# A scan's 32x32 inverse products broken into runs of 32 among projection matmuls

## The chip, the cores and the metric

The kernel runs on one core of a Trainium2 chip. The metric is the device time of one execution in microseconds, as the median of several executions.

## The reference

Four residual layers work on a sequence of 256 tokens of width 2048. Layers 0 and 3 are RWKV-7 time mixing, layer 1 is dilated attention, layer 2 a pooling mixer. Only the RWKV layers are touched. Cut to what matters:

```
def _rwkv7_mixer(h, ...):
    r, k, v, g = [(h + xx * mu[j]) @ w_in[j] for j in range(4)]
    decay = exp(-exp(w_log));  a = sigmoid(a0 + (xa @ a1) @ a2)
    kk = heads(k * k_k);  kk = kk / max(sqrt(sum(kk * kk)), 1e-12)
    k = k * (1 + (a - 1) * k_a)
    # S_t = S_{t-1} diag(w_t) + (S_{t-1} a_t) b_t^T + v_t k_t^T ;  y_t = S_t r_t
    y = _rwkv7_scan(r, decay, k, v, -kk, kk * a)
    y = _head_group_norm(y, lnx_w, lnx_b)
    bonus = sum(r * k * r_k, axis=-1) * v
    return ((y + bonus) * silu(g)) @ w_out
```

There are 32 heads of 64 channels. The recurrence over tokens is computed in 4 chunks of 64 tokens, and each chunk of each head needs the inverse of a 64x64 unit triangular matrix.

## The kernel before, in words

The four projections of an RWKV layer (r, k, v, g, each 2048 x 2048) are one long stream on TensorE. `linear` (L238) takes the weights in pieces of 512 KB: SyncE's queue loads `raw` (L190), ScalarE rounds it to `whi` (L193), VectorE makes the rest `wlo` (L194), and three matmuls of 256 columns per weight tile give a product (L284, tile `lin`). There are three buffers of each kind, and two pieces are fetched ahead. The inputs `xhi` and `xlo` (L169, L170) are made by `mix` from `hl`, read back from DRAM (L498, L502).

Everything else of the scan is written between the matmuls of that stream. `heads` and `group` are Python generators. After each step of six projection matmuls `linear` calls `tick`, which keeps a clock of its own: a generator yields (cost on TensorE in us, delay in us until its next piece may be written), or a letter for the stage it enters next and a condition for it. Stages A, S, D, C, E hold one generator each. A compiler pass then orders each engine's instructions by priority and by its own estimates. The engines work their lists in order and SyncE's queue is in order as well.

One `heads` generator handles a pair of blocks (4 heads): stage A makes decays and key norms (the products `z` L564, `ssp` L717), S the products inside a chunk (`sc` L771, L774; `tps` L796). Every second one goes on into `group` for 8 heads: stage D inverts, stage C runs the four chunks (`xps`, `ups`, `sps`, `yps`), E does the norm and the bonus (`gps` L970, `bps` L972, whose input `kb` is loaded at L967). A layer has 4 groups, the program 8.

In stage D the 16x16 diagonal blocks are inverted on VectorE, and TensorE joins them by products of 32x32 tiles: `prod` (L856, matmuls at L860) is called three times for tiles named `q`, then come `zp` (L876) and `pp` (L886). In `group` the second and third call stand back to back:

```
zp = prod(lambda o, n: NT[:, n, o % 64:o % 64 + 32], X0, 16)
yield 1.3, 2.0
...
xp = prod(lambda o, n: P0[:, n], Z, 32)
pp = prod(lambda o, n: Z[:, n], P0, 32)
yield 2.6, 2.5
```

A call of `prod` writes 64 matmuls of float32, and `zp` and `pp` 32 each. The trace records each such float32 matmul twice, so a call is 128 records there. A group's strictly triangular matrix `NT` has one buffer.

Of the kernel before, what the change touches and what calls it, by code (L numbers as in the profile page):

```python
# [9 lines left out]
F32 = mybir.dt.float32  # L10
F32R = mybir.dt.float32r
I32 = mybir.dt.int32
AF = mybir.ActivationFunctionType
ALU = mybir.AluOpType

P = 128
D = 2048
S = 256
# [4 lines left out]
C = 64  # L23
# [72 lines left out]
class Trunk:  # L96
# [482 lines left out]
    def rwkv(self, l, li):  # L579
        nc = self.nc  # L580
        a = self.i
        w2, srcs, have = {}, {}, (set(), set(), set(), set(), set(), set())
        self.omm = self.hid_pool.tile([P, 6 * KT], F32, name="omm")
        o = VIX[("mu", l, 0)] * KT
# [4 lines left out]
        io = lambda name: self.mp.tile([P, 2, S], F32, tag="io", name=name, bufs=4)  # L589
# [71 lines left out]
        with self.phase(f"scan{l}") as self.sp:  # L661

            grp = [[] for _ in range(KT // 4)]
            st = {"chunks": 0, "BK": False, "NT": None, "Y": False}
            self.queue += [(self.heads(l, li, pr, w2, srcs, have, grp[pr // 2], st),
                            lambda pr=pr: (2 * pr in have[0] and 2 * pr in have[1]
                                           and st["chunks"] >= pr // 2 - 1))
                           for pr in range(KT // 2)]
            for n, (m, lo, hi, rounds) in enumerate(self.order):
                xs = then[2]  # L670
                if n + 1 < len(self.order):
                    m2, lo2 = self.order[n + 1][:2]
                    then = (win(m2), lo2, self.mixer_inputs(l, m2), False)
                else:
                    then = (a["a_w_out"][l], 0,
                            lambda k: zs(k) if k // 2 * 2 in have[5] else None, True)
                self.part(win(m), lo, hi, xs, takes[m], rounds, then)
            self.drain()
# [3 lines left out]
    def heads(self, l, li, pr, w2, srcs, have, grp, st):  # L682


        nc, sp = self.nc, self.sp
        dma = nc.sync.dma_start
# [4 lines left out]
        j = 2 * pr  # L691

        sg = T("sg", [P, 4, S], 1)
        self.lora_out(sg[:, 0:2], w2["w"], j, srcs["w"], LORA_W, ("w0", l))
        self.lora_out(sg[:, 2:4], w2["a"], j, srcs["a"], LORA_W, ("a0", l))
        kt = T("kt", [P, 2, S], 1)
        dma(kt, self.kd[j // 2])
        yield 1.8, 1.5
        self.sigmoid_tail(sg)
        aa = sg[:, 2:4]  # L700
        Wi = T("Wi", [P, 2, S], 1)
# [10 lines left out]
        kk = T("kk", [P, 2, S], 1)  # L712
        for q in range(2):
            nc.scalar.activation(kk[:, q], kt[:, q], AF.Square, scale=self.col(("k_k", l), j + q))
        yield 0.0, 5.0
        ssp = self.ps.tile([P, 2, S], F32, tag="sm", name="ssp", bufs=2)
        nc.tensor.matmul(ssp.rearrange("p q t -> p (q t)"), self.cst("bd"),  # L717
                         kk.rearrange("p q t -> p (q t)"), start=True, stop=True)
# [12 lines left out]
        nc.vector.tensor_tensor(kp, kp, kt, op=ALU.mult)  # L731
        nc.vector.tensor_tensor(aa, aa, kk, op=ALU.mult)
        yield 0.9, 3.0
        while st["BK"]:
            yield 0.0, 1.0
        st["BK"] = True
        r = T("kt", [P, 2, S], 1)
        dma(r, self.rd[j // 2])
# [17 lines left out]

        mk = self.cst("smask")
        if pr % 2 == 0:
            while st["NT"] is not None:
                yield 0.0, 1.0  # L760
            st["NT"] = T("NT", [P, 16, C], 1)
        NT = st["NT"]
        n0 = pr % 2 * 8
        MR = T("MR", [P, 2, NC_, C], FLY)
        for q in range(2):
# [35 lines left out]
        st["BK"] = False  # L801
        grp.append((AR, MR, BT, Wc))
        if pr % 2:
            yield from self.group(l, li, pr // 2, have, grp, st)

    def group(self, l, li, gr, have, grp, st):

        nc, sp = self.nc, self.sp
        dma = nc.sync.dma_start
        T = lambda tag, shape, bufs: sp.tile(shape, F32, tag=tag, name=tag, bufs=bufs)  # L810
        half = (slice(0, 64), slice(64, 128))
        NT = st["NT"]

        yield "D", lambda: True
        ntd, pxd = self.ntd[gr % 2], self.pxd[gr % 2]
        for hh, rows in enumerate(half):
            dma(ntd[:, hh], NT[rows])
        Nb = T("Nb", [P, 16, 16], 1)
        for b in range(4):
            o = 16 * b  # L820
            dma(Nb[32 * b:32 * b + 32],
# [2 lines left out]
        px = px_.rearrange("p i (w t) -> p i w t", w=2)  # L824
        nc.scalar.copy(px[:, :, 0], self.cst("eye16").rearrange("p (i t) -> p i t", i=16))
        yield 0.0, 7.0
        tmp = T("tmp", [P, 64], 1)
        with self.tc.high_priority(PRIO_D):
            for i in range(15):
                w = 15 - i  # L830
# [14 lines left out]
        yield 0.0, 14.0  # L845

        rowm = self.cst("rows")
        PX = T("PX", [P, 16, 2, 32], 1)
        for o in range(2):
            nc.scalar.activation(PX[:, :, :, 16 * o:16 * o + 16],  # L850
                                 pc.rearrange("p (n w) t -> p n w t", w=2), AF.Copy,
# [1 line left out]
        P0, X0 = PX[:, :, 0], PX[:, :, 1]  # L853
        bank = lambda name: self.ps.tile([P, 16, 32], F32, tag="nt", name=name, bufs=2)

        def prod(fa, fb, kk_):  # L856
            q_ = bank("q")
            for n in range(16):
                for o in range(0, P, 32):
                    nc.tensor.matmul(q_[o:o + 32, n], fa(o, n)[o:o + kk_], fb[o:o + kk_, n],  # L860
                                     start=True, stop=True)
            return q_

        zp = prod(lambda o, n: NT[:, n, o % 64:o % 64 + 32], X0, 16)
        yield 1.3, 2.0
        Z = T("px", [P, 16, 32], 1)
        nc.scalar.activation(Z, zp, AF.Copy, scale=rowm[:, 1:2])
        xp = prod(lambda o, n: P0[:, n], Z, 32)
        pp = prod(lambda o, n: Z[:, n], P0, 32)
        yield 2.6, 2.5  # L870
        nc.vector.tensor_tensor(X0, X0, xp, op=ALU.add)
        nc.vector.tensor_tensor(P0, P0, pp, op=ALU.add)
        zp = bank("zp")
        for n in range(16):
            for b in (0, 64):
                nc.tensor.matmul(zp[b + 32:b + 64, n], NT[b:b + 32, n, 32:], X0[b:b + 32, n],  # L876
                                 start=True, stop=True)
        st["NT"] = None
        yield 1.0, 2.0
        Z2 = T("px", [P, 16, 32], 1)  # L880
        for b in (0, 64):
            nc.scalar.copy(Z2[b + 32:b + 64], zp[b + 32:b + 64])
# [1 line left out]
        for n in range(16):  # L884
            for b in (0, 64):
                nc.tensor.matmul(pp[b:b + 32, n], Z2[b + 32:b + 64, n], P0[b + 32:b + 64, n],  # L886
                                 start=True, stop=True)
        yield 1.0, 1.5
        yield "C", lambda: (4 * gr in have[2] and 4 * gr + 2 in have[2] and not st["Y"])
        Pm = T("P", [P, 16, C], 1)  # L890
        for o in range(2):
# [8 lines left out]
        def values(c):  # L900

            SV = T("SV", [P, 2, 2, 2, C], 2)
            UV = T("UV", [P, 2, 2, 2, C], 2)
            vc = vv[c * C:(c + 1) * C]
            for hh, rows in enumerate((half[1], half[0])):
                for t in (SV, UV):
                    dma(flat(t[rows, hh]), flat(vc[:, hh]))
            return SV, UV

        Y = T("Y", [P, 2, 2, S], 1)  # L910
        each = [(s, q, hh, rows) for s in range(2) for q in range(2)
# [5 lines left out]
        for c in range(NC_):  # L917
            xps = bank("xps")
            for s, q, hh, rows in each:
                nc.tensor.matmul(xps[rows, q, s], grp[s][0][:, hh, q, c, 0, :], SV[:, hh, q, s],  # L920
                                 start=True, stop=True)
            nxt = values(c + 1) if c < NC_ - 1 else None
            yield 0.5, 1.3
            X = T("X", [P, 2, 2, C], 1)
            nc.scalar.copy(X, xps)
            ups = bank("ups")
            for s, q, hh, rows in each:
                nc.tensor.matmul(ups[rows, q, s], Pm[rows, s * 8 + q * NC_ + c],
                                 X[rows, q, s], start=True, stop=True)
            yield 0.4, 1.6  # L930
            nc.vector.tensor_copy(UV[0:64, 0], ups[0:64])
            nc.scalar.copy(UV[64:128, 1], ups[64:128])
            if nxt:
                sps = bank("sps")
                for s, q, hh, rows in each:
                    nc.tensor.matmul(sps[rows, q, s], grp[s][2][:, hh, q, c],
                                     UV[:, hh, q, s], start=True, stop=True)
                for hh, rows in enumerate(half):
                    S_ = nxt[0][rows, hh]
                    nc.vector.tensor_tensor(S_, SV[rows, hh], sps[rows], op=ALU.add)  # L940
                    for s in range(2):
                        nc.vector.tensor_tensor(
                            S_[:, :, s], S_[:, :, s],
                            grp[s][3][rows, :, c:c + 1].broadcast_to([64, 2, C]), op=ALU.mult)
            yps = bank("yps")
            for s, q, hh, rows in each:
                nc.tensor.matmul(yps[rows, q, s], SV[:, hh, q, s], grp[s][0][:, hh, q, c, 1, :],
                                 start=(s == 0 and q == 0), stop=False, skip_group_check=True)
            for s, q, hh, rows in each:
                nc.tensor.matmul(yps[rows, q, s], UV[rows, hh, q, s], grp[s][1][rows, q, c],  # L950
                                 start=False, stop=True, skip_group_check=True)
            yield 1.6, 1.5
            st["Y"] = True
            nc.scalar.copy(Y[:, :, :, c * C:(c + 1) * C], yps)
            if nxt:
                SV, UV = nxt

        st["chunks"] += 1
        yield "E", lambda: True
        fl = lambda t: t.rearrange("p q t -> p (q t)")  # L960
        for s in range(2):
            j = 4 * gr + 2 * s
            y = Y[:, :, s]
            sq = T("gsq", [P, 2, S], 1)
            nc.scalar.activation(sq, y, AF.Square)
            v, kp = (self.mp.tile([P, 2, S], F32, tag="io", name=n, bufs=4) for n in ("v", "kb"))
            dma(kp, self.bd_[j // 2])  # L967
            dma(v, self.vd[l][j // 2])
            gps = self.ps.tile([P, 2, S], F32, tag="ch", name="gps", bufs=2)
            nc.tensor.matmul(fl(gps), self.cst("bd"), fl(sq), start=True, stop=True)  # L970
            bps = self.ps.tile([P, 2, S], F32, tag="ch", name="bps", bufs=2)
            nc.tensor.matmul(fl(bps), self.cst("bd"), fl(kp), start=True, stop=True)  # L972
            yield 1.8, 2.5
            nc.scalar.activation(sq, gps, AF.Ln, scale=1.0 / 64, bias=self.eps[:, 1:2])
            nc.scalar.activation(sq, sq, AF.Exp, scale=-0.5)
# [12 lines left out]
                have[5].add(j)  # L988
            else:
                dma(self.yd[j // 2], y)  # L990
            yield 0.0, 1.5
        st["Y"] = False


# [395 lines left out]
```

## Time and profile before

| | us |
|---|---|
| median of 3 executions | 2310.69 (2306.9 to 2314.41) |
| the profiled execution, its own time | 2314.95 |
| its span in the trace | 2313.2 |
| TensorE busy | 2194.3 (95%) |
| VectorE busy | 1510.2 (65%) |
| ScalarE busy | 1257.2 (54%) |
| the two scans in the trace | 205 to 663 and 1770 to 2237 |
| mean granted TensorE clock | 0.973 |

Times are read from the start of the span. A matmul's busy time is longer than the distance to the next one, since matmuls overlap, so rates are read from the distance between starts. "Idle before" is the time in which an engine had nothing to do before an instruction, and the name behind the arrow is what ended it. "issue" there means that the engine waited for nothing that the profile shows.

### The profile page before, as it was taken

To read this page: it belongs to the slowest core of one execution; us is meant where nothing else is said; L and a number is where in the kernel's file an instruction comes from. 1 tells how busy PE (TensorE), PEld (TensorE's weight loads), DVE (VectorE), ACT (ScalarE), POOL (GpSimd) and SP (SyncE) were. 2 spreads that over 40 slices of the span, in tenths; PEclk is the share of its full clock that TensorE was granted. 3 is DMA by queue.
4 is the path that set the end of the run, shared out by engine and by line. 5 is a ranking of instruction groups with operands and counts; after the bars stand their busy time and mean duration, and the time that the engine had idled before them with its cause. 6 is when DMAs were issued, how large, how long until landed. Compare 5 with 4: busy or idle time off the path is not lost.

```text
span 2313.2 us, 53463 instructions
## 1 busy us (share of the span) xinstructions
PE 2194.3 (95%) x22442; PEld 2026.7 (88%) x22442; DVE 1510.2 (65%) x2482; ACT 1257.2 (54%) x1850; POOL 4.6 (0%) x12
## 2 busy tenths in 40 slices
PE   7999898989899999999999999999999998989899
PEld 6998787878889888888899999998998887888889
DVE  7667677676456555655467675657668767685554
ACT  6556555555545544554456445545666655664542
POOL 0000000000000000000000000000000000000000
PEclk9999898989999999999999999999999999999999
DMA  7676776656666656456647556777586776675665
GB/s 258 220 252 206 228 222 203 201 182 197 192 216 203 189 185 190 144 165 190 191 129 241 178 183 218 246 222 229 163 293 221 233 227 199 206 219 164 200 202 168
DMA packets 230065, 472.69 MB, mean 204 GB/s; under 512 B 72000, under 2 KB 96192, under 8 KB 229824
## 3 DMA queue, kind: packets, MB, share of 16 engines
q1 hardware_dynamic: 199136, 441.30, 60.6%
q10 hardware_dynamic: 30048, 25.87, 3.5%
q8 instruction: 176, 2.88, 0.5%
q0 software_dynamic: 640, 2.10, 0.2%
q14 instruction: 65, 0.53, 0.1%
HBM read 414.66 MB, written 54.53 MB: 203 GB/s over the span
## 4 chain that ended last, share of the span: by engine, by line
PE 79%; DMA 8%; DVE 6%; issue 4%; ACT 3%; SPq 0%; ACTq 0%; POOL 0%; DVEq 0%; POOLq 0%
PE lin L284 47%; PE lin L318 17%; DMA hl<-hd 3%; DVE wlo L194 2%; PE u L539 1%; PE q L860 1%; DMA kb<-bd 1%; DMA raw<-in_a_w_in_dram 1%; PE z L564 1%; ACT whi L193 1%; PE sc L771 1%; PE yps L950 1%; DVE xlo L170 1%; PE xps L920 1%; DVE mt L502 1%
## 5 line engine op out<-in xcount | busy, mean ns | idle before, releaser
L284 PE MATMUL lin<-xhi,whi 128*128 128x256 f32 x3584 | 1054.8, 295 | 23.9 <-ACT xhi L169 23.5
L194 DVE TENSOR_TENSOR wlo<-raw,whi 128x1024 fp32r<-128x1024 f32 x600 | 733.5, 1224 | 489.4 <-ACT whi L193 481.4
L284 PE MATMUL lin<-xlo,whi 128*128 128x256 f32 x3584 | 1030.2, 288 | 6.1 <-DVE xlo L170 5.8
L284 PE MATMUL lin<-xhi,wlo 128*128 128x256 f32 x3584 | 1026.1, 287 | 0.9 <-DVE wlo L194 0.9
L193 ACT CAST whi<-raw 128x1024 fp32r<-128x1024 f32 x600 | 627.1, 1046 | 604.1 <-PE lin L284 381.7
L284 PEld LDWEIGHTS lin<-xhi,whi 128*128 128x128 f32 x3584 | 694.4, 194 | 47.9 <-ACT xhi L169 27.2
L284 PEld LDWEIGHTS lin<-xlo,whi 128*128 128x128 f32 x3584 | 696.0, 194 | 20.9 <-DVE xlo L170 9.6
L284 PEld LDWEIGHTS lin<-xhi,wlo 128*128 128x128 f32 x3584 | 695.5, 194 | 5.3 <-issue 2.4
L318 PE MATMUL lin<-whi,xhi 128*128 128x512 f32 x576 | 229.5, 399 | 0.0
L318 PE MATMUL lin<-whi,xlo 128*128 128x512 f32 x576 | 224.6, 390 | 0.0
L318 PE MATMUL lin<-wlo,xhi 128*128 128x512 f32 x576 | 224.4, 390 | 0.0
L318 PEld LDWEIGHTS lin<-whi,xlo 128*128 128x128 f32 x576 | 108.1, 188 | 22.7
L318 PEld LDWEIGHTS lin<-wlo,xhi 128*128 128x128 f32 x576 | 108.4, 188 | 20.9
L318 PEld LDWEIGHTS lin<-whi,xhi 128*128 128x128 f32 x576 | 108.3, 188 | 20.7
L502 DVE SCALAR_TENSOR_TENSOR mt<-hl,prm 128x256 f32<-128x256 f32 x152 | 70.4, 479 | 25.1 <-DMA hl<-hd 24.3
L169 ACT CAST xhi<-mt 128x512 fp32r<-128x512 f32 x96 | 58.8, 616 | 39.7 <-DVE mt L502 33.2
L170 DVE TENSOR_TENSOR xlo<-mt,xhi 128x512 fp32r<-128x512 f32 x96 | 65.5, 686 | 6.9 <-ACT xhi L169 6.3
L506 ACT ACTIVATE mt<-H,omm 128x256 f32<-128x256 f32 x120 | 54.1, 501 | 20.8 <-PE u L539 10.0
L508 DVE SCALAR_TENSOR_TENSOR mt<-H,prm,mt 128x256 f32<-128x256 f32 x120 | 52.9, 482 | 15.8 <-ACT mt L506 14.2
L783 DVE TENSOR_TENSOR AR<-sc,c 64x512 f32<-64x512 f32 x64 | 43.9, 685 | 25.1 <-PE sc L774 23.3
L539 PE MATMUL u<-l,mt 128*128 128x96 f32 (+1 forms) x320 | 42.3, 269 | 0.0
L771 PE MATMUL sc<-AR,BK 64*64 64x128 f32 x512 | 42.2, 289 | 0.1
(230 smaller groups left out, 2132.3 us busy)
## 6 DMA issues: line engine op xcount, KB each, us to landing
raw<-in_a_w_in_dram SPq DMA_DIRECT2D x256, 512.0 KB, 4.3
raw<-in_b_qkv_dram SPq DMA_DIRECT2D x144, 512.0 KB, 3.5
hl<-hd SPq DMA_DIRECT2D x152, 256.0 KB, 4.7
raw<-in_a_w_out_dram SPq DMA_DIRECT2D x64, 512.0 KB, 3.9
raw<-in_c_w_in_dram SPq DMA_DIRECT2D x64, 512.0 KB, 3.6
raw<-in_c_w_out_dram SPq DMA_DIRECT2D x32, 512.0 KB, 4.4
raw<-in_b_gate_dram SPq DMA_DIRECT2D x16, 512.0 KB, 3.5
raw<-in_b_w_out_dram SPq DMA_DIRECT2D x16, 512.0 KB, 4.7
```

Of the source, the lines that this page charges most:

```text
L169: nc.scalar.copy(hi, src)
L170: nc.vector.tensor_tensor(lo, src, hi.bitcast(F32), op=ALU.subtract)
L193: nc.scalar.copy(whi, raw)
L194: nc.vector.tensor_tensor(wlo, raw, whi.bitcast(F32), op=ALU.subtract)
L284: nc.tensor.matmul(ps[:, m], a, b, start=(k == 0 and m == 0 and q == 0), stop=(k == kt - 1 and q == 2), skip_group_check=True)
L318: nc.tensor.matmul(ps, a[:, sl], b[:, kk], start=(k == 0 and q == 0), stop=(k == KT - 1 and q == 2))
L502: nc.vector.scalar_tensor_tensor(t[:, q], h[q][:, 1], mu, h[q][:, 0], op0=ALU.mult, op1=ALU.add)
L506: nc.scalar.activation(t[:, q], self.H[:, k + q, 1:], AF.Copy, scale=self.omm[:, o:o + 1])
L508: nc.vector.scalar_tensor_tensor(t[:, q], self.H[:, k + q, 0:S], mu, t[:, q], op0=ALU.mult, op1=ALU.add)
L539: nc.tensor.matmul(u[:, tt], x[:, q, tt * P:(tt + 1) * P], wt[:, k + q], start=(k + q + tt == 0), stop=(k + q == KT - 1), skip_group_check ...
L771: nc.tensor.matmul(sb[rows, c], BK[rows, q, c, 0], AR[rows, hh, q, c], start=True, stop=True)
L783: nc.vector.tensor_tensor(AR[k, hh, q].rearrange("p c a t -> p c (a t)"), sk[k].rearrange("p c a t -> p c (a t)"), mk[k].unsqueeze(1).broa ...
```

## The change

- `prod` becomes a generator: a call's 64 matmuls are written as two runs of 32 with a yield between, and a yield stands between the calls too. `zp` and `pp` stay runs of 32, with smaller costs.
- `NT` gets a second buffer. `Nb` and `tmp` now lie in the buffer of `PX`, the squares `sq` in that of `P`.
- A pair may enter stage A before the groups two back have finished their chunks; that condition moves to the start of the second half of stage A.
- The two `lora_out` calls of stage A get a yield between them.
- The matmul for key norms is written 8 us after its inputs, in place of 5.
- The bonus product's inputs `kb` and `v` are loaded one step before the matmul that reads them.

```
-                            lambda pr=pr: (2 * pr in have[0] and 2 * pr in have[1]
-                                           and st["chunks"] >= pr // 2 - 1))
+                            lambda pr=pr: 2 * pr in have[0] and 2 * pr in have[1])
...
         self.lora_out(sg[:, 0:2], w2["w"], j, srcs["w"], LORA_W, ("w0", l))
+        yield 0.9, 1.5
         self.lora_out(sg[:, 2:4], w2["a"], j, srcs["a"], LORA_W, ("a0", l))
         kt = T("kt", [P, 2, S], 1)
         dma(kt, self.kd[j // 2])
-        yield 1.8, 1.5
+        yield 0.9, 1.5
...
-        yield 0.0, 5.0
+        yield 0.0, 8.0
         ssp = self.ps.tile([P, 2, S], F32, tag="sm", name="ssp", bufs=2)
...
-        while st["BK"]:
-            yield 0.0, 1.0
+        while st["BK"] or st["chunks"] < pr // 2 - 1:
+            yield 0.0, 0.5
...
-            while st["NT"] is not None:
-                yield 0.0, 1.0
-            st["NT"] = T("NT", [P, 16, C], 1)
-        NT = st["NT"]
+            while st["inv"] < pr // 2 - 1:
+                yield 0.0, 0.5
+            grp.append(T("NT", [P, 16, C], 2))
+        NT = grp[0]
...
-        Nb = T("Nb", [P, 16, 16], 1)
+        work = T("PX", [P, 1024], 1)
+        Nb = work[:, 0:256].rearrange("p (i t) -> p i t", i=16)
...
-        def prod(fa, fb, kk_):
-            q_ = bank("q")
+        def prod(q_, fa, fb, kk_):
+
             for n in range(16):
+                if n == 8:
+                    yield 0.5, 2.0
                 for o in range(0, P, 32):
                     nc.tensor.matmul(q_[o:o + 32, n], fa(o, n)[o:o + kk_], fb[o:o + kk_, n],
                                      start=True, stop=True)
-            return q_
-
-        zp = prod(lambda o, n: NT[:, n, o % 64:o % 64 + 32], X0, 16)
-        yield 1.3, 2.0
+
+        zp = bank("q")
+        yield from prod(zp, lambda o, n: NT[:, n, o % 64:o % 64 + 32], X0, 16)
+        yield 0.5, 2.5
         Z = T("px", [P, 16, 32], 1)
         nc.scalar.activation(Z, zp, AF.Copy, scale=rowm[:, 1:2])
-        xp = prod(lambda o, n: P0[:, n], Z, 32)
-        pp = prod(lambda o, n: Z[:, n], P0, 32)
-        yield 2.6, 2.5
+        xp, pp = bank("q"), bank("q")
+        yield from prod(xp, lambda o, n: P0[:, n], Z, 32)
+        yield 0.5, 2.0
+        yield from prod(pp, lambda o, n: Z[:, n], P0, 32)
+        yield 0.5, 2.5
...
+        def load(s):
+
+            v, kp = (self.mp.tile([P, 2, S], F32, tag="io", name=n, bufs=4) for n in ("v", "kb"))
+            dma(kp, self.bd_[2 * gr + s])
+            dma(v, self.vd[l][2 * gr + s])
+            return v, kp
...
-            yield 1.6, 1.5
             st["Y"] = True
+            if not nxt:
+                ld = load(0)
+            yield 1.6, 1.5
...
-            sq = T("gsq", [P, 2, S], 1)
-            nc.scalar.activation(sq, y, AF.Square)
-            v, kp = (self.mp.tile([P, 2, S], F32, tag="io", name=n, bufs=4) for n in ("v", "kb"))
-            dma(kp, self.bd_[j // 2])
-            dma(v, self.vd[l][j // 2])
+            y, sq = Y[:, :, s], sqs[:, s]
+            v, kp = ld
...
+            if s == 0:
+                ld = load(1)
+                nc.scalar.activation(sqs[:, 1], Y[:, :, 1], AF.Square)
             yield 1.8, 2.5
```

How the lists of instructions move. TensorE's list at the first inverse of the first scan, before (`q`, `zp` are the inverse's products, `sc` a product of the next pair, `lin` the projections):

```order
L284 MATMUL lin<-xlo,whi 128x256
L284 MATMUL lin<-xhi,wlo 128x256
L771 MATMUL sc<-AR,BK 64x128
L860 MATMUL q<-px,PX 32x32 x64
L860 MATMUL q<-PX,px 32x32 x64
L876 MATMUL zp<-PX,NT 32x32 x32
L771 MATMUL sc<-AR,BK 64x128
L774 MATMUL sc<-AR,BK 64x128 x2
```

The same inverse in the changed program, around one run of its third product:

```order
L284 MATMUL lin<-xhi,whi 128x256
L284 MATMUL lin<-xlo,whi 128x256
L284 MATMUL lin<-xhi,wlo 128x256
L862 MATMUL q<-PX,px 32x32 x32
L284 MATMUL lin<-xhi,whi 128x256
L284 MATMUL lin<-xlo,whi 128x256
```

The 160 products that stood in one block are now five runs of 32, and 24 projection matmuls stand between one run and the next here. The first call, 64 matmuls, still stands in one piece at this inverse.

At the third inverse of the first scan the changed list has this (`tps` are transposes of stage S):

```order
L284 MATMUL lin<-xhi,wlo 128x256
L796 MATMUL tps<-c_153,BK 64x64 x29
L862 MATMUL q<-PX,NT 32x32 x32
L796 MATMUL tps<-c_153,BK 64x64 x3
L862 MATMUL q<-PX,NT 32x32 x32
L284 MATMUL lin<-xhi,whi 128x256 x2
L284 MATMUL lin<-xlo,whi 128x256
```

There both runs of the first call still stand together, with the transposes directly ahead of them and no projection between.

SyncE's queue where the first group's bonus inputs are loaded, before:

```order
L907 DMA SV<-vcd 64x256
L967 DMA kb<-bd 128x512
L968 DMA v<-vd_76 128x512
L190 DMA raw<-in_a_w_in_dram 128x1024
L907 DMA UV<-vcd 64x256
```

and in the changed program:

```order
L844 DMA px<-pxd_89 16x512 x8
L917 DMA kb<-bd 128x512
L918 DMA v<-vd_76 128x512
L917 DMA kb<-bd 128x512
L918 DMA v<-vd_76 128x512
L753 DMA bd<-kp 128x512
L190 DMA raw<-in_a_w_in_dram 128x1024
```

The two pairs of loads, 11 rows apart before, now stand one behind the other in the queue.

## Rows read from the trace of the kernel before

**Rows 1.** Windows: busy time of each engine in the two scans.

```profile
core 0: us, PE busy (x) PEld busy (x) DVE busy (x) ACT busy (x) POOL busy (x), PEclk, DMA share, GB/s
...
205.00:663.00 458.00, 415.36 (x6338) 376.58 (x6336) 306.58 (x600) 258.03 (x403) 0.00 (x0) 0.94 0.66 202
...
1770.00:2237.00 467.00, 427.29 (x6381) 383.03 (x6379) 324.85 (x629) 275.00 (x436) 0.00 (x0) 0.95 0.66 206
```

**Rows 2.** TensorE's waits, whole span: line, what ended it, us, times, longest.

```profile
PE q L860 <- issue: 44.0, 16, 4.0
PE lin L284 <- ACT xhi L169: 23.5, 15, 5.8
...
PE bps L972 <- DMA kb<-bd: 6.9, 5, 2.1
PE ssp L717 <- ACT kk L714: 6.4, 2, 3.7
...
PE zp L876 <- issue: 2.7, 2, 1.7
```

**Rows 3.** TensorE's timeline at the first inverse: start, length, work, count, [idle before].

```profile
257.29 1.29 PE L860 MATMUL q<-PX,NT 16*32 16x32 f32 x128
258.51 0.39 PE L284 MATMUL lin<-xlo,whi 128*128 128x256 f32 x1
...
259.32 0.28 PE L284 MATMUL lin<-xlo,whi 128*128 128x256 f32 x1
259.44 0.28 PE L284 MATMUL lin<-xhi,wlo 128*128 128x256 f32 x1
...
261.20 0.62 PE L860 MATMUL q<-px,PX 32*32 32x32 f32 x49 [1.12 <-ACT px L867]
264.05 1.27 PE L860 MATMUL q<-px,PX 32*32 32x32 f32 x77 [2.23 <-issue]
265.08 0.24 PE L860 MATMUL q<-PX,px 32*32 32x32 f32 x1
265.09 0.24 PE L860 MATMUL q<-px,PX 32*32 32x32 f32 x2
265.14 0.84 PE L860 MATMUL q<-PX,px 32*32 32x32 f32 x48
269.97 1.12 PE L860 MATMUL q<-PX,px 32*32 32x32 f32 x68 [4.00 <-issue]
...
273.42 0.64 PE L876 MATMUL zp<-PX,NT 32*32 32x32 f32 x15 [1.00 <-issue]
...
276.49 0.41 PE L284 MATMUL lin<-xhi,wlo 128*128 128x256 f32 x1
276.70 0.41 PE L284 MATMUL lin<-xhi,whi 128*128 128x256 f32 x1
```

**Rows 4.** The page's busy times (TensorE's share, instructions) and its instruction queue (packets, MB).

```profile
PE 2194.3 (95%) x22442; PEld 2026.7 (88%) x22442; DVE 1510.2 (65%) x2482; ACT 1257.2 (54%) x1850; POOL 4.6 (0%) x12
...
q8 instruction: 176, 2.88, 0.5%
```

**Rows 5.** DMA queues from 257 to 274 us: the instruction queue.

```profile
q8 instruction: 3, 0.05, 1.1%
```

**Rows 6.** Windows: the first of eight stretches at half clock, and the sum of all.

```profile
263.70:277.40 13.70, 8.35 (x308) 7.69 (x309) 4.92 (x8) 3.99 (x8) 0.00 (x0) 0.50 0.62 217
...
sum 88.80, PE 62.26 PEld 57.77 DVE 30.54 ACT 24.94 POOL 0.00; mean PE 7.78 PEld 7.22 DVE 3.82 ACT 3.12 POOL 0.00
```

**Rows 7.** Windows: the same eight stretches, projection matmuls (L284) alone, the sum.

```profile
sum 88.80, PE 26.94 PEld 24.89; mean PE 3.37 PEld 3.11
```

**Rows 8.** Windows: after the key norms, at and after the first inverse.

```profile
157.90:164.70 6.80, 5.81 (x21) 4.78 (x22) 3.43 (x5) 6.62 (x11) 0.00 (x0) 0.50 0.34 108
257.30:263.70 6.40, 3.40 (x187) 2.87 (x187) 3.53 (x4) 3.42 (x4) 0.00 (x0) 1.00 0.97 293
277.40:290.00 12.60, 12.26 (x231) 11.34 (x231) 10.96 (x19) 6.54 (x12) 0.00 (x0) 1.00 0.52 169
```

More of the change, by code (lines that the diff above doesn't have):

```diff
@@ L663, in rwkv @@
             grp = [[] for _ in range(KT // 4)]
-            st = {"chunks": 0, "BK": False, "NT": None, "Y": False}
+            st = {"chunks": 0, "inv": 0, "BK": False, "Y": False}
             self.queue += [(self.heads(l, li, pr, w2, srcs, have, grp[pr // 2], st),
-                            lambda pr=pr: (2 * pr in have[0] and 2 * pr in have[1]
-                                           and st["chunks"] >= pr // 2 - 1))
+                            lambda pr=pr: 2 * pr in have[0] and 2 * pr in have[1])
                            for pr in range(KT // 2)]
@@ L803, in heads, with group @@
         if pr % 2:
-            yield from self.group(l, li, pr // 2, have, grp, st)
-    def group(self, l, li, gr, have, grp, st):
+            yield from self.group(l, li, pr // 2, have, NT, grp[1:], st)
+    def group(self, l, li, gr, have, NT, grp, st):
         nc, sp = self.nc, self.sp
@@ L811, in group @@
         half = (slice(0, 64), slice(64, 128))
-        NT = st["NT"]
         yield "D", lambda: True
@@ L826, in group @@
         yield 0.0, 7.0
-        tmp = T("tmp", [P, 64], 1)
+        tmp = work[:, 256:320]
         with self.tc.high_priority(PRIO_D):
@@ L847, in group @@
         rowm = self.cst("rows")
-        PX = T("PX", [P, 16, 2, 32], 1)
+        PX = T("PX", [P, 1024], 1).rearrange("p (n w t) -> p n w t", n=16, w=2)
         for o in range(2):
@@ L877, in group @@
                                  start=True, stop=True)
-        st["NT"] = None
-        yield 1.0, 2.0
+        st["inv"] += 1
+        yield 0.5, 2.0
         Z2 = T("px", [P, 16, 32], 1)
@@ L887, in group @@
                                  start=True, stop=True)
-        yield 1.0, 1.5
+        yield 0.5, 1.5
         yield "C", lambda: (4 * gr in have[2] and 4 * gr + 2 in have[2] and not st["Y"])
@@ L951, in group @@
                                  start=False, stop=True, skip_group_check=True)
+            st["Y"] = True
+            if not nxt:
+                ld = load(0)
             yield 1.6, 1.5
-            st["Y"] = True
             nc.scalar.copy(Y[:, :, :, c * C:(c + 1) * C], yps)
@@ L960, in group @@
         fl = lambda t: t.rearrange("p q t -> p (q t)")
+        sqs = T("P", [P, 16, C], 1).rearrange("p (s q c) t -> p s q (c t)", s=2, q=2)
+        nc.scalar.activation(sqs[:, 0], Y[:, :, 0], AF.Square)
+        yield 0.0, 1.0
         for s in range(2):
             j = 4 * gr + 2 * s
-            y = Y[:, :, s]
-            sq = T("gsq", [P, 2, S], 1)
-            nc.scalar.activation(sq, y, AF.Square)
-            v, kp = (self.mp.tile([P, 2, S], F32, tag="io", name=n, bufs=4) for n in ("v", "kb"))
-            dma(kp, self.bd_[j // 2])
-            dma(v, self.vd[l][j // 2])
+            y, sq = Y[:, :, s], sqs[:, s]
+            v, kp = ld
             gps = self.ps.tile([P, 2, S], F32, tag="ch", name="gps", bufs=2)
@@ L990, in group @@
                 dma(self.yd[j // 2], y)
-            yield 0.0, 1.5
+        yield 0.0, 2.0
         st["Y"] = False
```

## Prediction

> **What bounds the kernel now.** I read the windows by stage first, then TensorE's waits, then the timeline at one inverse, then the clock. In the two scans TensorE is busy 415.4 of 458 us and 427.3 of 467 us [rows 1], VectorE about 0.67 and 0.70 of the time, the DMA engines 0.66. So TensorE bounds both scans, and what can be won there without less work is its idle time, 42.6 + 39.7 = 82.3 us, and time at a low clock. The waits name the largest part: matmuls of `q` wait 44.0 us and those of `zp` 2.7 us for "issue", that is for nothing the profile shows as a semaphore [rows 2]. That is 46.7 of the 82.3 us, in 18 waits at 8 inverses.
>
> The timeline tells what it is [rows 3]. The first product, 128 records, runs through in 1.3 us. The next run stops after 49 records for 2.23 us, goes on for 77 + 1 + 2 + 48 = 128 records, stops for 4.00 us, and stops once more before `zp`. From one of those stops to the next is exactly 128 records. The page counts 22442 matmuls and as many weight loads, and 176 packets on the instruction queue [rows 4]: 44884 / 176 = 255 instructions, so one packet is 128 matmul records with their weight loads. Three such packets fall into the 17 us around the inverse [rows 5], where the mean over the span is one in 13.1 us. **The engine runs out of instructions**: small products use up a packet in 1.3 us, and the next comes 5.92 us (264.05 to 269.97) or 3.45 us (to 273.42) after the last. One packet in hand covers the first product, not the three packets in one block behind it. Projections use 128 records in 128 x 0.12 = 15 us (259.32 to 259.44 is one step) and never run dry.
>
> [...]
>
> [...]
>
> **The change, part by part.**
>
> *Runs of 32 with projections between.* 160 products that stood in one block now stand in five runs with 24 projections between. A run is 64 records in 0.65 us, 24 projections take 24 x 0.12 = 2.9 us: 88 records in 3.5 us, so a packet lasts 5.1 us. Starved, packets came at 3.45 to 5.92 us, and one is in hand at the start. So most stops go. Two places keep some: the first call in one piece at the first inverse, and the third inverse, where transposes and 64 products stand together. I leave 6 us of the 46.7: **-41 us**; bounds 0 (not the fetch) and -47.
>
> *The clock there.* If it fell because of the stops, 23 us come back, less a little where stops are left: **-22 us**; bounds 0 and -31.
>
> *More switches.* After a run the first projection takes 0.39 us in place of 0.28 [rows 3], and I put as much on the way in: 0.2 us a switch. Four more runs at 8 inverses are 32 switches: **+6 us**; bounds +3 and +10.
>
> *Key norms 8 us after their inputs.* `ssp` waits 6.4 us in two places [rows 2], and the first is followed by 6.8 us at half clock with 5.81 us of work [rows 8]. In the changed list 48 more projections (5.8 us) stand ahead of the first `ssp`, more than its longest wait of 3.7 us. The wait goes, -6 us, and about 3 us of clock with it: **-9 us**; bounds 0 and -11.
>
> *Bonus inputs one step ahead.* The matmul waits 6.9 us for `kb` in five places [rows 2]. The loads now stand 1.6 us of planned TensorE work and a step earlier: **-5 us**; bounds 0 and -7. Both pairs of loads then hold four of the four `io` buffers, so a load behind them in SyncE's queue can wait for one; weights are fetched two pieces ahead, 2 x 24 x 0.12 = 5.8 us, which covers a wait of up to that. If the cover is gone, the price is in the next term.
>
> *What is late next.* The 28.7 us of other waits in the scans (82.3 - 46.7 - 6.9) are mostly projections waiting for `xhi`, 23.5 us over the whole span [rows 2]. Each engine behind TensorE now gets some 7% less time for the same work, and the stops no longer let it catch up. I add a quarter and a little: **+8 us**; bounds 0 and +29 (they double).
>
> *`NT`'s second buffer, the moved condition, the split `lora_out`.* The first inverse moves back by 57 projections and the last one forward by some 250 in the lists, so that the last group's chunks have about 144 projections of the layer behind them where they had 30. That shortens a tail in which TensorE hardly waits now, so I cost it at nothing; covered by the chunk work of the group before. `Nb` in `PX`'s buffer makes its load wait for the copies that read `PX`; SyncE's queue holds the next weights behind that, under the same 5.8 us of cover: nothing.
>
> The sum is -41 - 22 + 6 - 9 - 5 + 8 = -63 us. The profiled execution took 2314.95 us, so 2252 us; it lies 4.3 us above the median of the runs shown, so I forecast a median of **2248 us**, 2.7% below. Its own range is 2228 to 2270.
>
> **The rivals.**
>
> *Given back elsewhere (faster, less so).* TensorE reaches its inputs earlier than VectorE and the DMA queue deliver them. For it: VectorE at 0.70 and DMA at 0.66 already, 15 waits for `xhi`. Against it: VectorE still has a quarter of either scan free, and the projections are fetched ahead. With other waits doubled and more (+30 on the sum): 2278 us.
>
> [...]
>
> *The change doesn't reach the stops.* If "issue" is not the fetch, only key norms and bonus inputs are won: -9 - 5 + 6 = -8, so 2307 us, 2303 us as a median. Against it stand the 128 records. That the runs would not be spread at all is excluded by the list of instructions.
>
> **How the numbers follow.** The forecast's case has 0.69, given back 0.17, slower 0.05, not the fetch 0.05, and 0.04 is for more than forecast, below 2228 us (all terms at their good ends). The range 2226 to 2288 us takes in the first case and most of the second, and leaves out some 0.17. About 0.3%, 7 us, is what a measurement of this kernel can tell from no change. Faster by more than that: 0.69 + 0.17 + 0.04 and about half of "not the fetch" (2303 us lies at the edge), 0.92. Within it: 0.03. Slower: 0.05.
>
> **What would show it.** In the changed profile the waits of `q` for "issue" should fall from 44.0 to below 8 us, the granted clock of the scans rise from 0.94 and 0.95 to about 0.99, `ssp` and `bps` vanish from the waits or stay below 2 us each, and each scan shorten by about 30 us, while the stages outside keep their length. The forecast is wrong if the issue waits stay; if they go and the clock stays at half around the runs; or if waits for `xhi` grow by more than 30 us.

## The result, and the profile after

| | before | changed |
|---|---|---|
| median of 4 executions each, same chip, us | 2312.55 (2306.9 to 2316.44) | 2281.7 (2277.67 to 2284.83) |
| ratio to before | | 0.9868 [0.984, 0.9895] |
| profiled execution, its span, us | 2313.2 | 2281.2 |
| mean granted TensorE clock | 0.973 | 0.980 |

The changed kernel is 31 us faster, 1.3%. The forecast was 63 us: 2281.7 lies inside the range, 34 us above 2248.

The first view is the windows of the two kernels, cut where the same number of matmuls of tile `lin`, the projections of all layers, has been issued (860, 3202, 9694 and 12107 of 12672, one or two more in the changed kernel), so that each row holds the same work (those of [rows 1] are cut by time): scan 1, the layers between, scan 2, the rest. Before:

```profile
core 0: us, PE busy (x) PEld busy (x) DVE busy (x) ACT busy (x) POOL busy (x), PEclk, DMA share, GB/s
144.10:656.40 512.30, 465.41 (x6806) 422.51 (x6805) 346.53 (x661) 295.36 (x460) 0.00 (x0) 0.94 0.66 203
656.40:1713.70 1057.30, 1049.59 (x7154) 975.25 (x7153) 661.23 (x918) 541.72 (x741) 4.45 (x8) 1.00 0.63 199
1713.70:2240.50 526.80, 483.31 (x6909) 435.23 (x6908) 367.44 (x690) 314.96 (x496) 0.00 (x0) 0.95 0.67 208
```

The changed kernel, same cuts:

```profile
144.20:631.80 487.60, 463.09 (x6807) 418.33 (x6806) 348.24 (x661) 295.40 (x460) 0.00 (x0) 0.97 0.69 214
631.80:1687.50 1055.70, 1048.99 (x7154) 974.85 (x7153) 660.95 (x918) 543.30 (x742) 4.45 (x8) 1.00 0.63 199
1687.50:2208.50 521.00, 487.35 (x6909) 438.53 (x6908) 367.77 (x691) 315.38 (x496) 0.00 (x0) 0.96 0.68 210
```

Scan 1 is 24.7 us shorter, scan 2 only 5.8, where some 30 each were forecast; the layers between keep their length. In scan 2 TensorE's idle time (span less busy) fell from 43.5 to 33.7 us, but its busy time for the same matmuls rose by 4.0 us.

TensorE's waits in the changed kernel, whole span, answer to [rows 2]:

```profile
PE lin L284 <- ACT xhi L169: 12.6, 6, 5.8
...
PE sc L771 <- ACT sg L567: 5.2, 4, 2.2
PE q L862 <- issue: 5.0, 3, 3.1
PE sc L771 <- DVE AR L748: 4.8, 6, 1.2
...
PE vps L620 <- DVE rvo L612: 4.4, 4, 2.5
PE pp L890 <- ACT px L886: 3.9, 4, 1.0
PE lin L284 <- ACT whi L193: 3.3, 2, 2.2
PE lin L284 <- issue: 3.0, 1, 3.0
...
PE tps L796 <- DVE MR L778: 2.7, 2, 2.4
...
PE ups L939 <- ACT X L936: 2.4, 1, 2.4
PE sc L774 <- ACT sg L567: 1.9, 3, 0.8
```

"issue" is 8.6 us in all, from 46.7. The waits of `ssp`, and of `bps` for `kb`, are gone, and waits for `xhi` nearly halved. New are many waits of 1 to 2.5 us at small products: `sc`, `pp`, `tps`, `ups`, more at `vps`. Over the program the idle time of TensorE between matmuls fell by 33.5 us: issue -38.1, `ssp` -6.9, `bps` -6.8, all others together +18.3.

Of the 15 stretches at half clock between 150 and 2250 us I show two and the sum, which answers to [rows 6]:

```profile
185.70:192.50 6.80, 6.46 (x43) 5.57 (x44) 5.73 (x11) 5.26 (x9) 0.00 (x0) 0.50 0.78 255
...
1858.20:1865.10 6.90, 6.17 (x42) 5.22 (x44) 2.12 (x3) 3.27 (x9) 0.00 (x0) 0.51 0.48 167
...
sum 81.80, PE 73.77 PEld 68.20 DVE 53.02 ACT 43.18 POOL 0.00; mean PE 4.92 PEld 4.55 DVE 3.53 ACT 2.88 POOL 0.00
```

The same sum of the kernel before, over its 14 stretches between the same times (the eight of [rows 6] and six more):

```profile
sum 116.10, PE 87.13 PEld 79.22 DVE 51.18 ACT 46.73 POOL 0.00; mean PE 6.22 PEld 5.66 DVE 3.66 ACT 3.34 POOL 0.00
```

The stretches lost 34.3 us, but 20.9 of these were idle time; the work done at half clock fell by 13.4 us only (87.13 to 73.77). At half clock a projection step of the kernel before took 0.21 us (276.49 to 276.70) where it takes 0.12 (259.32 to 259.44) at a granted clock of 1.00, and 128 records of products 1.93 us (264.05 to 265.98) in place of 1.29 [rows 3]. From these four times I estimate that between a third and 0.43 of such work is lost, so the clock gave back 4.5 to 5.7 us, not 25 (22 at the inverses, 3 at the key norms).

One such place shows where it comes from. ScalarE in the changed kernel, timeline at 177 to 188 us:

```profile
182.90 0.51 ACT L714 ACTIVATE kk<-kt,prm 128x256 f32<-128x256 f32 x1 [4.40 <-DMA kt<-kd]
...
185.17 0.82 ACT L567 ACTIVATE sg<-z,zb 128x256 f32<-128x256 f32 x2
```

And TensorE there:

```profile
179.74 1.13 PE L564 MATMUL z<-lsw,l 96*128 96x256 f32 x4
...
182.87 1.03 PE L564 MATMUL z<-lsa,l 96*128 96x256 f32 x4
186.04 1.97 PE L771 MATMUL sc<-AR,BK 64*64 64x128 f32 x16 [2.15 <-ACT sg L567]
```

ScalarE stood 4.40 us on `kt`, the load for the key norms' squares `kk`. The `sg` that reads the two `z` products stood behind it in ScalarE's list, though it needs no `kt`. And `sc` needs `sg`, though it doesn't read it: the tiles `z`, `ssp`, `sc` and `tps` share two buffers of the kernel's PSUM pool (`bufs=2`), and a pair of `sc` tiles takes both, each once `sg` has read the `z` that lies in it. `sc` waited 2.15 us for `sg` and then ran 1.97 us per 16 at a granted clock of 0.50, where the same matmuls take 1.09 us at full clock (at 1730.5, granted 1.00, and in e16, below). ScalarE's waits name the resource:

```profile
ACT kk L714 <- DMA kt<-kd: 35.3, 13, 4.4
```

Before it was 23.7 us in 11 waits. Seven of the 13 are followed within 4 us by a wait of TensorE of about 1 us or more that ScalarE ended: `lin` at 159.8 and 1704.1, `sc` at 186.0, 225.7, 463.0 and 1730.5, `ups` at 1858.9. At four of these the clock fell, at 161.8, 185.7, 1704.6 and 1858.2, for 3.4 to 6.9 us; at the other three it didn't.

Why `kt` came late here stands on VectorE's and SyncE's timelines:

```profile
175.81 0.88 DVE L751 SCALAR_TENSOR_TENSOR kp<-kt,prm,kp 128x256 f32<-128x256 f32 x2
...
177.13 0.43 SPq L697 DMA_DIRECT2D kt<-kd  x1
```

`kt` has one buffer, and the `r` of the pair before lies in it until VectorE has read it, to 176.69. SyncE issued the load 0.44 us later, and a load of `kt` takes 2.8 to 5.2 us to land. In 8 of the 16 pairs the load is issued less than 0.5 us after that last read; in the others the buffer was free earlier. That the wait for `kt` costs time is what the experiments had to show.

### The profile page after: what moved, and what is told of

Same layout as the page of the kernel before. It is cut to its first block, busy times and chain, and to the rows that moved or that the text cites. A ratio compares the mean times of both kernels' runs of the same rounds, so it can differ in the third digit from the quotient of the medians.

```text
span 2281.2 us, 53422 instructions
## 1 busy us (share of the span) xinstructions
PE 2195.8 (96%) x22442; PEld 2025.7 (89%) x22442; DVE 1510.8 (66%) x2482; ACT 1258.5 (55%) x1850; POOL 4.7 (0%) x12
## 5 line engine op out<-in xcount | busy, mean ns | idle before, releaser
L284 PE MATMUL lin<-xhi,whi 128*128 128x256 f32 x3584 | 1061.1, 297 | 16.1 <-ACT xhi L169 12.6
L284 PE MATMUL lin<-xhi,wlo 128*128 128x256 f32 x3584 | 1025.9, 287 | 7.7 <-DVE wlo L194 4.8
L284 PE MATMUL lin<-xlo,whi 128*128 128x256 f32 x3584 | 1027.9, 287 | 2.7 <-DVE xlo L170 2.7
L284 PEld LDWEIGHTS lin<-xhi,whi 128*128 128x128 f32 x3584 | 695.5, 194 | 41.0 <-ACT xhi L169 14.3
L284 PEld LDWEIGHTS lin<-xlo,whi 128*128 128x128 f32 x3584 | 696.9, 195 | 12.7 <-issue 7.0
L284 PEld LDWEIGHTS lin<-xhi,wlo 128*128 128x128 f32 x3584 | 695.9, 194 | 8.9 <-DVE wlo L194 6.2
L169 ACT CAST xhi<-mt 128x512 fp32r<-128x512 f32 x96 | 58.5, 617 | 34.3 <-DVE mt L502 23.5
L783 DVE TENSOR_TENSOR AR<-sc,c 64x512 f32<-64x512 f32 x64 | 43.9, 686 | 10.6 <-PE sc L774 9.6
L771 PEld LDWEIGHTS sc<-AR,BK 64*64 64x64 f32 x512 | 30.5, 140 | 16.6 <-ACT sg L567 7.1
```

The lines of the kernel that those rows point to most:

```text
L169: nc.scalar.copy(hi, src)
L284: nc.tensor.matmul(ps[:, m], a, b, start=(k == 0 and m == 0 and q == 0), stop=(k == kt - 1 and q == 2), skip_group_check=True)
L771: nc.tensor.matmul(sb[rows, c], BK[rows, q, c, 0], AR[rows, hh, q, c], start=True, stop=True)
L783: nc.vector.tensor_tensor(AR[k, hh, q].rearrange("p c a t -> p c (a t)"), sk[k].rearrange("p c a t -> p c (a t)"), mk[k].unsqueeze(1).broa ...
```

## The experiments

Ratios are to the kernel before, run on the same chip, with a 95% interval; a point is one per cent of that kernel's time. The edit is against the changed kernel where nothing else is said.

**The runs of 32.** The kernel before with nothing but the runs:

```
+            for n in range(16):
+                if n == 8:
+                    yield 0.5, 2.0
...
+        yield from prod(xp, lambda o, n: P0[:, n], Z, 32)
+        yield 0.5, 2.0
+        yield from prod(pp, lambda o, n: Z[:, n], P0, 32)
+        yield 0.5, 2.5
```

> The kernel before with the runs of 32 alone (one NT buffer, old conditions, old steps of stage A). Theory W (new waits): the fetch stops fall from 46.7 us to about 20, since in the lists the last inverse of each scan now comes after the projections have run out; waits of sc and tps for sg stay at before's level (under 1 us in all) and the half-clock stretches at the first three inverses of a scan go, so about 2290 us. Theory P (the 32x32 products themselves hold the clock at half): each inverse keeps some 10 us or more at half clock although its stops are gone, 2305 us or more.

Measured: 2323.84 us, 1.0017 [0.9997, 1.0037]. TensorE's waits:

```profile
PE lin L284 <- ACT xhi L169: 25.9, 11, 5.8
PE ssp L717 <- ACT kk L714: 12.2, 5, 4.2
PE q L862 <- issue: 12.0, 6, 2.7
...
PE gps L974 <- ACT gsq L969: 6.8, 4, 2.3
```

Most stops went here too ("issue" 14.9 us in all, from 46.7) and nothing was won: waits of `ssp` and `gps` took their place, and the last inverse of each scan slid to the end of the projections, so that few stood between its runs (clock 0.73 in 575 to 625 us of the first scan). Removing the stops is not enough.

The opposite, the changed kernel with calls of 64 in one piece (`if n == 8` never taken):

> The changed kernel without the yield in the middle of a product, so runs of 64. Fetch theory: a run is one whole instruction packet, and at several places two stand close together, so the waits for issue rise from 8.6 us to about 30 (25 to 42), and the time to about 2300 us. If the number of switches between small and large matmuls is what costs, the time falls by 3 us or more in place.

Measured: 2296.42 us, 0.9898 [0.9863, 0.9932]. Its waits:

```profile
PE q L862 <- issue: 20.3, 13, 4.6
...
PE lin L284 <- issue: 4.4, 2, 2.6
```

With longer blocks the stops return ("issue" 26.7 us in all), as the reading of the prediction has it. The time alone wouldn't show it: the interval overlaps that of the changed kernel.

**Why `sc` waits for `sg`.** First the moved condition put back:

```
-                            lambda pr=pr: 2 * pr in have[0] and 2 * pr in have[1])
+                            lambda pr=pr: (2 * pr in have[0] and 2 * pr in have[1]
+                                           and st["chunks"] >= pr // 2 - 1))
...
-        while st["BK"] or st["chunks"] < pr // 2 - 1:
+        while st["BK"]:
```

> The changed kernel with the condition on the chunks back at the start of stage A. Theory W: with stage A no longer early, waits of sc and tps for sg fall by half or more (from 9.0 us), but the last chunks of each scan lie beyond the projections again, so 2275 to 2285 us. If instead the moved condition has nothing to do with these waits, they stay at 9 us and the later end costs 5 us or more: 2287 us.

Measured: 2290.53 us, 0.9874 [0.9847, 0.9902]; `sc` waits 8.4 us for `sg`. So the condition isn't what makes `sc` wait. Then `kt`'s load ahead of both `lora_out`:

> The changed kernel with the load of kt issued ahead of the two lora_out calls. Theory W, in its form that ScalarE stands at the squares kk, waits there for kt, and so keeps the sg behind it from freeing the PSUM banks that sc needs: sc's waits for sg fall from 7.1 us to under 2, and with the clock behind them the time falls by 6 to 12 us, to about 2272 us. If the banks are the limit without kt, nothing changes by more than 3 us.

Measured: 2281.28 us, 0.9831 [0.98, 0.9862]; `sc` waits 6.9 us for `sg`, and ScalarE 33.6 us for `kt`; the interval overlaps that of the changed kernel. The load now stands ahead of both `lora_out` in the program, but it still waits for the buffer:

```profile
174.36 0.88 DVE L751 SCALAR_TENSOR_TENSOR kp<-kt,prm,kp 128x256 f32<-128x256 f32 x2
...
175.68 0.38 SPq L694 DMA_DIRECT2D kt<-kd  x1
```

Again 0.44 us lie between VectorE's last read (to 175.24) and the issue, and again this is so in 8 of the 16 pairs. So e4 didn't bring `kt` earlier, and can't show what an earlier `kt` would give. Then the two `lora_out` in one step again:

```
         self.lora_out(sg[:, 0:2], w2["w"], j, srcs["w"], LORA_W, ("w0", l))
-        yield 0.9, 1.5
         self.lora_out(sg[:, 2:4], w2["a"], j, srcs["a"], LORA_W, ("a0", l))
...
-        yield 0.9, 1.5
+        yield 1.8, 1.5
```

> The changed kernel with the two lora_out calls of stage A in one step again. Theory S: the second z, which now comes right ahead of the next sc, holds both banks that sc needs, so with one step the waits of sc for sg fall from 7.1 us to under 2 us, and the whole gains 8 us or more: ratio to before 0.983 or lower. If it is the denser program as a whole that makes sc wait, the waits of sc stay above 5 us, and the ratio at 0.985 to 0.989.

Measured: 2265.78 us, 0.9769 [0.9744, 0.9795], a point better than the changed kernel, and no wait of `sc` for `sg` is left. So the split, which the prediction put at nothing, costs a point here. The split alone, in the kernel before:

> The kernel before with one edit: a yield between the two lora_out calls of stage A. Theory S (the split puts the second z right ahead of a product that needs its bank): waits of sc or tps for sg of 4 us or more appear where before had none, and the time rises by 5 to 20 us, ratio 1.002 to 1.009. If the split only hurts together with the moved condition or the second NT buffer, no such wait shows and the ratio is 0.997 to 1.002.

Measured: 2337.2 us, 1.0093 [1.0067, 1.0119]. A point there too, but not by that wait:

```profile
PE q L861 <- issue: 37.8, 16, 5.1
...
PE bps L973 <- DMA kb<-bd: 10.2, 4, 4.1
...
PE sps L937 <- DVE UV L932: 6.1, 3, 4.4
PE vps L620 <- ACT rvo L604: 5.2, 2, 5.0
...
PE sc L775 <- ACT sg L567: 0.2, 1, 0.2
```

The waits that grew against before are those of `lin` for `wlo` (+6.5 us), `vps` (+6.0), `bps` (+3.3) and `sps` (+3.2). Neither expectation is met: the time rose, but without the waits of `sc` or `tps` for `sg` that theory S asked for.

To test the wait for `kt` itself, the split stays and the squares leave ScalarE (e16):

```
-            nc.scalar.activation(kk[:, q], kt[:, q], AF.Square, scale=self.col(("k_k", l), j + q))
+            nc.gpsimd.tensor_scalar(kk[:, q], kt[:, q], self.col(("k_k", l), j + q), None,
+                                    op0=ALU.mult)
+        nc.gpsimd.tensor_tensor(kk, kk, kk, op=ALU.mult)
```

> The changed program, with the squares for the key norms made on GpSimd (two multiplications by the key scale and one square) in place of ScalarE; nothing else differs. In the changed kernel ScalarE's list has these squares ahead of the sigmoid inputs sg of the same pair, and ScalarE stands on them until kt has landed (35.3 us in 13 waits over the program), while matmuls of sc wait for sg (7.1 us) because a product's bank is not yet read. Theory (the wait for kt in ScalarE's list is what delays sg, and through it sc): the waits of sc for sg fall from 7.1 us to under 2 us, the half-clock stretch behind 186 us goes, and the time falls to 2255 to 2270 us where before takes 2312, a ratio of 0.976 to 0.982. Rival (the split of lora_out costs through the places of z and sg in the lists, whatever kt does): the waits of sc for sg stay above 5 us and the ratio stays at 0.986 to 0.989. A third way: GpSimd is slow at it and the matmul ssp waits for kk, by more than 10 us in all; then the ratio is above 0.989 and the two cannot be told apart by the time, only by the waits of sc.

Measured: 2259.06 us (2256.17 to 2261.7), 0.9747 [0.9726, 0.9769], the fastest of all. Windows with the same cuts:

```profile
144.10:623.80 479.70, 457.77 (x6806) 414.01 (x6805) 352.18 (x661) 290.61 (x444) 28.73 (x24) 0.98 0.71 217
...
1677.60:2181.70 504.10, 480.19 (x6909) 431.65 (x6908) 370.34 (x691) 309.14 (x480) 31.56 (x24) 0.98 0.71 217
```

What is left of TensorE's waits:

```profile
PE q L864 <- issue: 5.2, 3, 2.9
...
PE sc L776 <- ACT sg L567: 2.1, 2, 1.3
```

The place of the 2.15 us on its timeline:

```profile
181.45 1.09 PE L773 MATMUL sc<-AR,BK 64*64 64x128 f32 x16
184.47 1.09 PE L776 MATMUL sc<-AR,BK 64*64 64x128 f32 x16 [1.26 <-ACT sg L567]
```

None of the four half-clock stretches named above is left; some waits of `sc` for its other input, VectorE's `AR`, stay. The scans are 32.6 and 22.7 us shorter than before. With the wait for `kt` out of ScalarE's list the profiled span is 27 us shorter (2281.2 to 2254.4), where the forecast's sum had missed 31. Half of it, 13.3 us, is idle time of TensorE: the waits that ScalarE ended fell from 36.2 to 21.5 us (`sc` for `sg` -5.0, `lin` for `whi` -3.3, `ups` -2.4, `lin` for `xhi` -2.3, `tps` -1.9), those that VectorE ended rose by 3.1. The other half, 13.4 us, is busy time of TensorE for the same matmuls: the half-clock stretches add up to 51.2 us in place of 81.8. The edit also changes the order of the lists, and e9 (above) and e17 (below) move the time by 0.9 and 0.65 points where the wait of `sc` for `sg` doesn't explain it, so how much of the 27 us is the wait alone isn't separated. GpSimd takes 978 ns (median) for one multiplication of 128x256, ScalarE 506 ns for a whole square of that size; `ssp`, written 8 us after, doesn't notice.

Is the split's cost that wait and no more? Squares on GpSimd and the two `lora_out` joined:

> The changed program with the key norms' squares on GpSimd and, on top, the two lora_out in one step again. The squares alone gave 0.9747, joining lora_out alone 0.9769, the changed kernel 0.9868. Theory (the split costs only because sg then stands behind ScalarE's wait for kt): with that wait gone the split costs nothing, so joining them again changes nothing: ratio 0.972 to 0.978. Rival (the split has a cost of its own, one point, as it had in the kernel before): the gains add, ratio 0.963 to 0.968, some 2235 to 2245 us.

Measured: 2272.19 us, 0.9812 [0.9794, 0.9831]: slower than the squares alone, and against joining alone (e3) the intervals just meet. The rival, a cost of the split's own, is refuted here, but so is the theory's "nothing": with the wait gone, the split gains 0.65 points. Its `issue` waits are 11.0 us at `q` and 3.1 at `sc`, `ssp` waits 3.8.

Did the kernel before pay for the same wait? Its squares on GpSimd:

> The kernel before with the key norms' squares on GpSimd and nothing else. There ScalarE stood on kt for 23.7 us in 11 waits, but sc waited for sg for no more than 0.1 us. Theory (the wait for kt costs where something that TensorE wants soon stands behind it, which the change brought about): little is won, ratio 0.996 to 1.002, while the issue waits of q stay at 40 to 46 us. Rival (ScalarE's wait cost the kernel before as much): ratio 0.986 to 0.990, as the squares on GpSimd gave the changed kernel (0.9747 against 0.9868).

Measured: 2344.5 us, 1.0123 [1.0104, 1.0143], outside both expectations. There `ssp` comes 5 us after and can't hide GpSimd:

```profile
PE ssp L719 <- POOL kk L716: 12.8, 5, 4.8
...
PE zp L878 <- issue: 9.0, 5, 2.3
```

So this run doesn't answer its question, which stays open.

**The other parts.** Key norms 5 us after their inputs, as before:

> The changed kernel with key norms 5 us after their inputs again. The forecast's term: the waits of ssp for kk come back (6 to 12 us) and each brings some us of half clock, ratio 0.990 to 0.993. If the later key norms only put off the wait to the instructions behind, the ratio stays within 0.985 to 0.989.

Measured: 2291.12 us, 0.9879 [0.9848, 0.991], no difference that shows; `ssp` waits 2.3 us in two places. The later matmul as such is worth little here. The run is also a warning for the account above: ScalarE waited 23.0 us for `kt` in place of 35.3 and `sc` 3.5 us for `sg` in place of 7.1, and the time didn't fall, since waits for `xhi` (+8.4) and for "issue" (+5.0) stood in their place.

The waits of `pp` and `vps`: `pp` 4 us after `zp` in place of 2, `vps` 2 to 3 us later:

```
-            self.active.append([turn(), "T", None, self.now + (1.0 if l == 0 else 3.0)])
+            self.active.append([turn(), "T", None, self.now + (3.0 if l == 0 else 6.0)])
...
-        yield 0.5, 2.0
+        yield 0.5, 4.0
```

> The changed kernel with pp written 4 us after zp in place of 2, and the centred values vps 2 and 3 us later. Theory C1 (short waits of TensorE let the clock fall): the waits of pp for px (3.9 us) and of vps for rvo (6.8 us) go, and with them the half-clock stretches behind them (at 390, 500 and 1954 us in the changed kernel), so 6 to 10 us of waits and 6 us of clock: ratio 0.981 to 0.984. Theory C2 (the products hold the clock down): these stretches stay at the inverses though nothing waits there, ratio 0.985 or more.

Measured: 2275.41 us, 0.9813 [0.9787, 0.984]; `pp` waits 0.7 us, `vps` 2.1 for `rvo`, and the half-clock stretches behind those waits, at 390.5 and 499.7, are gone. The third one that the expectation names, at 1954, is half as long (1956.3 to 1959.7), now behind a wait of `z` of 1.7 us, and the one at the first inverse is twice as long, 13.7 us from 280.3, with waits of 2.7 us of `q` ahead of it and of `lin` in it. Half a point is won; the intervals just meet. With e3's edit on top:

> Both edits of e3 and e7 together. If the waits they take away are independent, the gains add: ratio 0.976 to 0.981. If each wait that goes only shows the next, the ratio is no lower than the better of the two.

Measured: 2264.44 us, 0.9773 [0.9741, 0.9806]: nothing beyond e3, since `z` now waits 10.7 us for `MR`. Two more on top of e3 ask about the planner's cost of a run (1.0 in place of 0.5) and the moved condition:

> The kernel of e3 with each run of 32 products entered at a cost of 1.0 us in place of 0.5, so that less other small work is written beside it. Fetch theory: the issue waits left in e3 (12.4 us) stand where runs meet sc and tps, and fall to 5 to 9 us; ratio 0.972 to 0.977. If those places are made by the ordering pass and not by the costs, the waits stay at 10 us or more and the ratio at 0.977 or above.

Measured: 2278.25 us, 0.9834 [0.981, 0.9858], 0.65 points slower than e3, with `q` still at 10.6 us of "issue".

> The kernel of e3 with the condition on the chunks back at the start of stage A. With the split gone, the moved condition is worth what the earlier inverses save at the ends of the scans: if that is something, ratio 0.979 to 0.984, else as e3, 0.975 to 0.979.

Measured: 2288.82 us, 0.9884 [0.986, 0.9909], with 22.4 us of "issue" at `q` in 10 waits. The moved condition is worth 1.15 points beside joined `lora_out` (e11 less e3) and nothing beside split ones (e2).

## Why the prediction was wrong

- *Fetch, -41: right.* "Issue" fell by 38.1 us, and e5 brings 18 us of it back. The 8.6 us left lie where runs stand too close. The two largest in the changed kernel, on TensorE's timeline of the first inverse and the fifth:

```profile
269.13 1.16 PE L796 MATMUL tps<-c,BK 64*64 64x64 f32 x64
270.22 0.38 PE L284 MATMUL lin<-xhi,whi 128*128 128x256 f32 x1
271.10 1.29 PE L862 MATMUL q<-PX,NT 16*32 16x32 f32 x128 [0.50 <-ACT PX L850]
...
276.02 0.37 PE L284 MATMUL lin<-xhi,wlo 128*128 128x256 f32 x1 [2.96 <-issue]
...
1839.16 0.44 PE L862 MATMUL q<-PX,px 32*32 32x32 f32 x15 [3.12 <-issue]
```

  "Issue" followed how the products stand: 46.7 us with the blocks of the kernel before, 8.6 with the products spread, 26.7 with calls of 64 (e5). That the engine runs out of instructions there is inferred from stops 128 records apart [rows 3] and 44884 / 176 = 255 instructions to a packet [rows 4]; no run shows when a packet reaches the engine.
- *Clock, -22, and 3 of the key norms' 9: wrong, and this is the first step that failed:* "If it fell because of the stops, 23 us come back". No run shows these 23 us, nor the 22 of the sum that rest on them: they were the author's estimate. What the runs showed in their place: the clock did fall at the stops (to 0.50 at 263.7, within the stop of 2.23 us that ends at 264.05 [rows 3, rows 6]), but by the estimate above 4.5 to 5.7 us came back in place of 25, since in the changed kernel it falls as well behind other waits, of 0.7 to 2.5 us: 11 of the 15 stretches stand there, three at the stops that are left, and one, at 1557.9, outside the scans as before. When e7 took away two such waits, the stretches behind them went. That the products themselves hold the clock down (theory P of e1, C2 of e7) is refuted: the fourth inverse, runs and all, keeps a granted clock of 1.00 and no idle time, and so does the eighth (2105 to 2150 us, 45.00 us busy at 1.00):

```profile
540.00:590.00 50.00, 50.00 (x925) 45.55 (x926) 27.15 (x40) 27.92 (x41) 0.00 (x0) 1.00 0.62 196
```

- *"The split `lora_out`": "I cost it at nothing". This is the second step that failed.* The prediction gave a reason for the other two edits of that term and none for the split, and didn't ask what stands behind ScalarE's squares in its list. Joining (e3) was worth 23 us, taking the squares out (e16) 28. The moved condition, in the same term, was worth nothing beside the split (e2) and 1.15 points without it (e11); `NT`'s second buffer wasn't measured apart.
- *What is late next, +8: measured +18.3,* on other work than forecast: `xhi` fell by 10.9 us, while `sc` rose by 11.9, `tps` 4.9, `vps` 4.1, `pp` 3.9, `ups` 2.5 and `xps` 1.9. The prediction took the 28.7 us of other waits in the scans to be mostly for `xhi`, from a row over the whole span. In its two scan windows `xhi` is only 12.8 us:

```profile
PE lin L284 <- ACT xhi L169: 6.1, 5, 1.7
PE lin L284 <- ACT xhi L169: 6.7, 7, 2.3
```

- *Key norms, the wait: gone from `ssp` as forecast (-6.9), but not its cause.* ScalarE stood on `kt` for longer, 35.3 us against 23.7, and other work paid. e6 shows the term at next to nothing.
- *Bonus inputs, -5: right.* `bps` 6.9 to 0.2.
- *Switches, +6:* not measured apart. What remains of the 32.0 us of span after idle time (-33.5) and clock (-4.5 to -5.7) is +6 to +7.

Set against the sum, 63 us forecast and 32 us of span measured, the 31 us that are missing are some 20 us of clock, 10 us of late work and 3 us of fetch, less 3 us that `bps` and `ssp` gave beyond their terms.

*Given back elsewhere*, 2278 us, was the rival that came true, by another road than `xhi`. What stays open: what a buffer of its own for `kt`, apart from `r`, would give, which no run tests; and how much of e3 and e16 is the wait and how much the new order of the lists. The effects don't add (e8, e17, e2 with e11), so no single edit has a price that holds in another order.

## What to carry to other kernels

Break a block of small matmuls only where large ones stand between the pieces ("issue" fell here from 46.7 us to 8.6), and count what then stands directly before each piece. When a step is cut in two, read the in-order list of every engine that reads its result: here an instruction that waited for a DMA held what stood behind it (4.40 us for `kt`, with `sg` behind), and its move to an idle engine was worth nearly as much as the change itself (28 us against 31, though the order of the lists moved with it); in the kernel before, where `ssp` waited 12.8 us for the slower engine, the same move lost 1.2% (e18). Ask also what holds that DMA back: in e4 the load of `kt`, written ahead of both `lora_out`, was still issued 0.44 us after the last read of its buffer, at 175.68. Value a lost stop with its clock only if no other wait will stand in its place (4.5 to 5.7 us came back here, of 25).

## What the runs showed of the hardware

Among small products, half clock followed even short waits: `q` waited 0.69 us at 470.1 and the clock fell at 472.4; `pp` waited 1.01 us twice at 497.5 and 498.7 and it fell at 499.7, each time to 0.50 or 0.51 for 3.4 us. It didn't follow every wait: `sc` waited 1.0 us at 225.7, 463.0 and 1730.5, and no stretch at half clock came there: the granted clock is 1.00 in 225 to 232, 463 to 470 and 1730 to 1738 us. And the order of the lists alone moves this kernel by a point with the same arithmetic on every engine, in either direction: 1.0093 against before (e9), 0.9769 against 0.9868 (e3).
